# Sample's value products alternate the heads, and the layer norms' partial sums are added on VectorE

## The chip, the cores and the metric

The kernel runs on one core of a Trainium2 chip. The metric is the device time of one execution in microseconds. The engines are called by their names in the profile: PE (TensorE, matrix products; PEld its weight loads), DVE (VectorE), ACT (ScalarE), POOL (GpSimd) and SP (SyncE, which issues the DMAs). Each works through its own queue in program order, and semaphores order the queues against each other.

## What is computed

One step of a streaming encoder layer, for 512 prompt rows and 64 sample rows with a cache of 128 rows, model width 1024. Two groups of eight heads of width 64 attend: one with a forget gate and a causal mask, one over rows that an indexer picks. Then follow an output projection, a layer norm, a squared-ReLU feed-forward part of width 4096, a second layer norm and a gate.

```python
def layer_norm(x, g, b):
    mu = jnp.mean(xf, axis=-1, keepdims=True)
    var = jnp.mean(jnp.square(xf - mu), axis=-1, keepdims=True)
    return ((xf - mu) * lax.rsqrt(var + LN_EPS) * g + b).astype(x.dtype)
...
x = layer_norm(ALPHA * x + jnp.einsum('blm,md->bld', mix, w_o), ln1_g, ln1_b)
hid = jnp.square(jax.nn.relu(jnp.einsum('bld,df->blf', x, w_up)))
x = layer_norm(ALPHA * x + jnp.einsum('blf,fd->bld', hid, w_down), ln2_g, ln2_b)
```

Sample's attention of one head ends in probabilities (64 queries by 128 cached and 64 new rows) times values: `o = P[:, :128] @ V_cache + P[:, 128:] @ V_new`.

## The kernel before

All 576 rows lie along the free dimension and the 1024 features along the partitions, in eight blocks of 128: a tensor such as `Y` is [128, 8, 576]. Large products take float32 operands as a rounded part and a rest (`AH`/`AL`, `BH`/`BL`, the weights `whl`), three products for one; they are the products of line 273 in `gemm`. The products of the layer norms and of sample's attention take plain float32.

**Attention.** The projections of a pair of heads run on PE, and between their products the stages of the pair before are dealt out: scores (`qk`), bias and maximum, exponentials, transposes of the probabilities, values (`pv`), evacuation. The eight pairs are eight times the same pattern. `pv` writes one PSUM tile `V` (one buffer), head 0 to partitions 0 to 63, head 1 to 64 to 127. For the prompt (line 903) it alternates the heads inside the loop over key blocks. For the sample it does head 0, then head 1: each with a product over 128 cached rows (line 894, `Vc`) that begins the sum and one over 64 new rows (line 896, `vs`) that ends it.

**Layer norm.** The class `LayerNorm` does one half of the rows: L1A and L1B for the first norm (288 rows each, LN1), L2A (256) and L2B (320) for the second (LN2). A mean over features is a mean over 8 blocks and 128 partitions. `add` sums the blocks two by two into `self.s`, called `ln_s` in the profile, [128, 2, w], as they come out of the projection (lines 1100 and 1102, on DVE for L1A and the last pair, else on POOL); a product with the constant matrix `onesm` (1/1024 everywhere) sums over partitions and, with two accumulating products, over the two columns of partial sums:

```python
for x in range(2):
    PE.matmul(mu, onesm, self.s[:, x], start=(x == 0), stop=(x == 1))
```

`steps` then subtracts the mean in four steps (DVE, line 1128), squares (ACT, 1130 and 1133) and sums the squares into the same tile (line 1134, DVE or POOL). For the variance the tile is the weights of the product and one column of `onesm` streams through (line 1142), for each block of up to 128 rows and both partial sums. A square root (ACT), a reciprocal (DVE, 1148), a transpose that spreads the result over the partitions (line 55), scaling (1157) and the two parts `BH` (ACT, 1161) and `BL` (DVE, 1165) follow. The first half of `up(0)`, the up-projection, starts with these.

While L1A and L1B run, PE does the end of the output projection (`wo2`, evacuated by DVE at line 1208), then `ple` (products `g<-pT`, evacuated by ACT at line 1221), then `up(0)`; DVE also splits weights (line 179). In LN2 it is the last down-projection and the gate. A scheduler takes the operations in the order of the program and places them on the engines' queues by when it reckons their inputs ready, so that a change of one step can move its neighbours.

Of the kernel before, what the change touches and what calls it, by code (L numbers as in the profile page):

```python
# [11 lines left out]
OP = mybir.AluOpType  # L12
# [23 lines left out]
def tile_hybrid_step(ctx: ExitStack, tc: tile.TileContext, I, O):  # L36
    nc = tc.nc
    PE, ACT, DVE, POOL, SP = nc.tensor, nc.scalar, nc.vector, nc.gpsimd, nc.sync
# [4 lines left out]
    def f(ap):  # L43
        return ap.bitcast(F32)
# [5 lines left out]
    onesm = base.tile([128, 128], F32, name="onesm")  # L50
# [3 lines left out]
    def transpose(out, in_, n):  # L54
        PE.transpose(out, in_, ident[:n, :n])  # L55
# [58 lines left out]
    class Weights:  # L114
# [9 lines left out]
        def add(self, ap, pool_l=False, pair=None):  # L124
            aps = [ap] if pair is None else [ap, pair]
            n = 2 if pair is None else 7
            self.items.append(dict(aps=aps, h0=self.nh, n=n, pool=pool_l, left=None, when=0))
            self.nh += n
            return len(self.items) - 1
# [53 lines left out]
        def pieces_of(self, it, views):  # L183
# [24 lines left out]
            def add(x, out, a, b):  # L208
                return h0 + x, lambda: DVE.tensor_tensor(out, a, b, OP.add)

            t0 = add(3, tot[:, 0], b12, b22)
            t1 = add(2, tot[:, 1], b11, tot[:, 0])
            t2 = add(4, tot[:, 2], b21, tot[:, 1])
            t3 = add(5, b12, b12, b11)
# [83 lines left out]
    def psum_1(tag, bufs, dt=F32):  # L298
        return psA.tile([128, 512], dt, name=tag, tag="V" if tag == "V" else "R", bufs=1 if tag == "V" else 3)
# [586 lines left out]
    def pv(j):  # L886
        P = pair[j["p"]]
        ps = psum_1("V", 1)
        j["O"] = ps
        if j["s"]:  # L890
            g, pp = divmod(j["p"], 4)
            for hh in range(2):
                r = slice(hh * 64, hh * 64 + 64)
                PE.matmul(ps[r, :NS], Vc[g][:, (2 * pp + hh) * 64:(2 * pp + hh + 1) * 64], j["PT"][:, 0, r],
                          start=True, stop=False)
                PE.matmul(ps[r, :NS], P["vs"][:, r], j["PT"][:NS, 1, r], start=False, stop=True)
            return
        i = j["i"]
        for kb in range(i + 1):
            c = slice(0, 256) if kb < i else slice(128, 256)  # L900
            for hh in range(2):
                r = slice(hh * 64, hh * 64 + 64)
                PE.matmul(ps[r, c], P["vt"][:, kb, r], j["PT"][:, hh, kb, c], start=(kb == 0), stop=(kb == i))  # L903
# [16 lines left out]
    def jobs_of(p):  # L920
# [3 lines left out]
    PLAN = (((oevac, 5), (addmax, 1), (exp, 2), (make_bias, 0), (make_bias, -1)),  # L924
            ((ptrans, 3), (norm, 2)),
            ((qk, 0), (pevac, 3), (scales, 3), (pv, 4)))

    all_jobs = [j for p in range(8) for j in jobs_of(p)]
# [5 lines left out]
    def ticks(n):  # L934

        for _ in range(n):
            t = tick_no[0]
            tick_no[0] += 1
            for micro in PLAN:
                for stage, lag in micro:  # L940
                    j = job(t - lag)
                    if j and (j["close"] or stage not in (pv, oevac)) and not (stage is make_bias and "bias" in j):
                        stage(j)
                yield 1
# [132 lines left out]
    def psum_n():  # L1077
        return psN.tile([128, 512], F32, name="n", tag="n", bufs=2)
# [3 lines left out]
    class LayerNorm:  # L1082
# [10 lines left out]
        def add(self, j):  # L1093

            y = Y[:, :, self.sl]
            self.sums = j
            if j == 0:
                self.s = fb.tile([128, 2, 320], F32, name="ln_s", tag="ln_s" if self.sl.start else "relu", bufs=1 if self.sl.start else 2)[:, :, :self.w]
            elif j == 2:
                (DVE if self.sl is A else POOL).tensor_tensor(self.s, y[:, 0:2], y[:, 2:4], OP.add)  # L1100
            else:
                (DVE if j == 6 or self.sl is A else POOL).tensor_tensor(self.s, self.s, y[:, j:j + 2], OP.add)

        def pump(self):
            return next(self.gen, 0)
# [9 lines left out]
        def steps(self):  # L1115
            sl, gi, w = self.sl, self.gi, self.w
            y = Y[:, :, sl]
            while self.sums < 6:
                yield 1
            for _ in range(self.waits[0]):  # L1120
                yield 1
            mu = psum_n()[:, :w]
            for x in range(2):
                PE.matmul(mu, onesm, self.s[:, x], start=(x == 0), stop=(x == 1))  # L1124
            mb = mu[:, None, :].to_broadcast([128, 2, w])
            ss = self.s
            for j in range(0, 8, 2):
                DVE.tensor_tensor(y[:, j:j + 2], y[:, j:j + 2], mb, OP.subtract)
                if j == 0:
                    ACT.activation(ss, y[:, 0:2], AF.Square)  # L1130
                else:
                    sq = fb.tile([128, 2, 320], F32, name="ln_sq", bufs=2)[:, :, :w]
                    ACT.activation(sq, y[:, j:j + 2], AF.Square)
                    (DVE if j == 6 or sl is A else POOL).tensor_tensor(ss, ss, sq, OP.add)
                yield 1
            for _ in range(self.waits[1]):
                yield 1
            blks = [(c, min(128, w - c)) for c in range(0, w, 128)]
            var = psum_n()
            for i, (c, n) in enumerate(blks):  # L1140
                for x in range(2):
                    PE.matmul(var[:n, i:i + 1], ss[:, x, c:c + n], onesm[:, 0:1], start=(x == 0), stop=(x == 1))
            rt = fb.tile([128, 4], F32, name="ln_r", bufs=2)
            for i, (c, n) in enumerate(blks):
                if i == 0 or n < 128:
                    m = len(blks) - (blks[-1][1] < 128) if i == 0 else i + 1
                    ACT.activation(rt[:n, i:m], var[:n, i:m], AF.Sqrt, bias=epst[:n, 0:1])
                    DVE.reciprocal(rt[:n, i:m], rt[:n, i:m])
            for _ in range(self.waits[2]):
                yield 1  # L1150
            rb = psum_n()[:, :w]
            for i, (c, n) in enumerate(blks):
                transpose(rb[:, c:c + n], rt[:n, i:i + 1].to_broadcast([n, 128]), n)

            def scale(j):
                for x in (j, j + 1):
                    DVE.scalar_tensor_tensor(y[:, x], y[:, x], gb[:, gi, x:x + 1], rb, op0=OP.mult, op1=OP.mult)

            def high(j):
                for x in (j, j + 1):  # L1160
                    ACT.activation(BH[:, x, sl], y[:, x], AF.Identity, bias=gb[:, gi + 1, x:x + 1])

            def low(j):
                for x in (j, j + 1):
                    DVE.scalar_tensor_tensor(BL[:, x, sl], y[:, x], gb[:, gi + 1, x:x + 1], f(BH[:, x, sl]),
                                             op0=OP.add, op1=OP.subtract)
                self.ready += 1

            def bias(j):
                for x in (j, j + 1):  # L1170
                    ACT.activation(y[:, x], y[:, x], AF.Identity, bias=gb[:, gi + 1, x:x + 1])

            scale(0)
            high(0)
            yield 1
            scale(2)
            high(2)
            low(0)
            yield 1
            for j in (4, 6):  # L1180
                scale(j)
                high(j)
                yield 1
                low(j - 2)
                yield 1
            low(6)
            yield 1
            for _ in range(self.waits[3]):
                yield 1
            for j in range(0, 8, 2):  # L1190
                bias(j)
                yield 1

    def wo2(hs, ln, steps):
        for j in range(0, 8, 2):
            m = psum_g()
            for x in range(2):
                cs = slice((j + x) * 128, (j + x + 1) * 128)
                for k in (6, 7):
                    W = unit_w(U["ok", k], U["ok", 6])  # L1200
                    for _ in gemm(m[:, x, :HW], W, (0,), BH[:, k:k + 1], BL[:, k:k + 1], hs,
                                  first=(k == 6), last=(k == 7), wc=cs):
                        pass
                WT.step(steps)
                yield 1

            def ev(j=j, m=m):
                DVE.tensor_tensor(Y[:, j:j + 2, hs], m[:, :, :HW], Y[:, j:j + 2, hs], OP.add)
                ln.add(j)
            later(0, ev)  # L1210
# [341 lines left out]
```

## Time and profile before

| | before |
|---|---|
| median of 3 runs, us | 805.97 (805.49 to 806.9) |
| profiled execution, us | 805.3 |
| its span, us | 803.6 |
| granted TensorE clock | 1.00 in all stretches |
| records of sample's value products | 32 (line 894) and 32 (line 896) |
| records of the mean and the variance | 16 (line 1124) and 44 (line 1142) |

A row of the timeline has the start, the time from the first start to the last end, the engine, the line, the operation, output and inputs with shapes, and the number of records that it merges; for a product "128*64" is the part of the array used, rows by columns. In square brackets stands the idle time of the engine before it and who ended it. A row of the stretches has the stretch and its length, then busy time (and records) of PE, PEld, DVE, ACT and POOL, the clock and the use of DMA.

### The profile page before, as it was taken

What the parts mean: (1) busy time and instruction counts of PE and PEld (TensorE: products, weight loads), DVE (VectorE), ACT (ScalarE), POOL (GpSimd) and SP (SyncE); (2) the same over time, 40 slices, a digit from 0 to 9 for tenths busy, and PEclk for the clock granted to TensorE, in tenths of its full rate; (3) what the DMA queues carried; (4) which work ended last, traced back from release to release, by engine and by line L of the source; (5) the groups of instructions that cost most, each with busy time, mean ns of one, the idle gap of its engine ahead of it and who ended that gap; (6) DMA issues with size and microseconds to landing.
All of it is one profiled execution on the core that took longest, in us unless ns stands there. A gap on an engine that the chain in (4) does not pass through costs nothing.

```text
span 803.6 us, 14983 instructions
## 1 busy us (share of the span) xinstructions
PE 790.7 (98%) x5916; PEld 761.6 (95%) x5916; DVE 538.7 (67%) x1098; ACT 430.0 (54%) x905; POOL 120.0 (15%) x117
## 2 busy tenths in 40 slices
PE   7999999999999999999999999999999999999997
PEld 7988898999999999999999999999999999999997
DVE  6689999554456554989755858577594765647553
ACT  5568665767767544497424427154372534626351
POOL 8203435354332000110000000000000000012200
PEclk9999999999999999999999999999999999999999
DMA  8436233253222223442412314132231422630001
GB/s 295 167 55 151 90 106 94 87 191 122 86 72 84 73 73 117 151 163 60 125 53 80 105 53 131 53 106 82 77 106 53 132 80 79 245 109 27 27 28 65
DMA packets 30214, 81.44 MB, mean 101 GB/s; under 512 B 5056, under 2 KB 8896, under 8 KB 30016
## 3 DMA queue, kind: packets, MB, share of 16 engines
q1 hardware_dynamic: 30144, 80.49, 31.8%
q8 instruction: 46, 0.75, 0.4%
q14 instruction: 24, 0.20, 0.1%
HBM read 66.38 MB, written 9.54 MB: 94 GB/s over the span
## 4 chain that ended last, share of the span: by engine, by line
PE 86%; DVE 6%; issue 5%; ACT 1%; POOL 1%; DMA 0%; DVEq 0%; ACTq 0%; POOLq 0%
PE g L273 54%; PE m L273 17%; PE n L273 2%; PE V L903 2%; PE T L55 2%; DVE m L632 1%; DVE dbias L634 1%; PE S L818 1%; PE S L820 1%; PE m L413 1%; PE X L55 1%; PE S L420 1%; PE m L420 1%; PE n L1124 0%; DVE whl L179 0%
## 5 line engine op out<-in xcount | busy, mean ns | idle before, releaser
L175 ACT CAST whl<-wraw 128x512 fp32r<-128x512 f32 (+1 forms) x214 | 127.6, 611 | 142.4 <-PE g L273 116.2
L273 PE MATMUL g<-BH,whl 128*128 128x288 f32 (+2 forms) x864 | 181.9, 297 | 0.1
L273 PE MATMUL m<-AH,whl 128*128 128x288 f32 x736 | 177.9, 309 | 0.0
L179 DVE TENSOR_TENSOR whl<-wraw,whl 128x512 fp32r<-128x512 f32 (+1 forms) x180 | 121.3, 696 | 54.4 <-ACT whl L175 51.7
L273 PEld LDWEIGHTS g<-BH,whl 128*128 128x128 f32 x864 | 141.1, 188 | 2.4 <-ACT u L1318 1.2
L273 PEld LDWEIGHTS m<-AH,whl 128*128 128x128 f32 x736 | 126.3, 188 | 3.6 <-issue 2.2
L273 PE MATMUL g<-BL,whl 128*128 128x288 f32 (+2 forms) x432 | 127.2, 295 | 0.0
L273 PE MATMUL m<-AL,whl 128*128 128x288 f32 x368 | 109.0, 296 | 0.0
L273 PE MATMUL g<-hidE,whl 128*128 128x288 f32 (+2 forms) x768 | 103.4, 295 | 0.0
L273 PE MATMUL g<-hidO,whl 128*128 128x288 f32 (+2 forms) x768 | 103.4, 295 | 0.0
L273 PEld LDWEIGHTS g<-hidO,whl 128*128 128x128 f32 x768 | 102.4, 188 | 0.0
L273 PEld LDWEIGHTS g<-hidE,whl 128*128 128x128 f32 x768 | 102.2, 188 | 0.1
L273 PEld LDWEIGHTS g<-BL,whl 128*128 128x128 f32 x432 | 81.3, 188 | 0.1
L273 PEld LDWEIGHTS m<-AL,whl 128*128 128x128 f32 x368 | 69.6, 189 | 0.4
L273 PE MATMUL g<-s,whl 128*128 128x288 f32 x432 | 68.5, 298 | 0.0
L273 PEld LDWEIGHTS g<-s,whl 128*128 128x128 f32 x432 | 60.1, 188 | 2.2 <-DVE u L1320 1.2
L1100 POOL TENSOR_TENSOR ln_s<-Y 128x576 f32<-128x576 f32 (+2 forms) x3 | 4.6, 1544 | 383.8 <-DVE Y L1382 371.4
L179 POOL TENSOR_TENSOR whl<-wraw,whl 128x512 fp32r<-128x512 f32 x34 | 44.9, 1320 | 82.5 <-ACT whl L175 67.0
L836 ACT ACTIVATE sP<-sP,st 128x128 f32<-128x128 f32 (+4 forms) x72 | 39.6, 551 | 29.9 <-DVE st L828 29.3
L175 ACT CAST whl<-wsum 128x512 fp32r<-128x512 f32 x36 | 22.2, 616 | 60.7 <-PE g L273 60.5
L1357 DVE SCALAR_TENSOR_TENSOR Y<-Y,g 128x576 f32<-128x576 f32 x48 | 36.1, 751 | 24.5 <-PE g L273 24.0
L273 PE MATMUL m<-BH,whl 128*128 128x288 f32 x192 | 43.5, 304 | 0.0
(275 smaller groups left out, 1273.7 us busy)
## 6 DMA issues: line engine op xcount, KB each, us to landing
wraw<-in_w_up_dram SPq DMA_DIRECT2D x32, 512.0 KB, 3.5
wraw<-in_w_down_dram SPq DMA_DIRECT2D x32, 512.0 KB, 3.5
wraw<-in_w_qkv_dram SPq DMA_DIRECT2D x23, 512.0 KB, 4.1
wraw<-in_w_gate_dram SPq DMA_DIRECT2D x8, 512.0 KB, 4.6
wraw<-in_w_o_dram SPq DMA_DIRECT2D x8, 384.0 KB, 3.0
out_vT_dram<-v SPq DMA_DIRECT2D x8, 288.0 KB, 2.3
Y<-in_xT_dram SPq DMA_DIRECT2D x8, 288.0 KB, 5.5
PLD<-PL SPq DMA_DIRECT2D x4, 576.0 KB, 2.8
```

Source lines behind the costliest of these rows:

```text
L55: PE.transpose(out, in_, ident[:n, :n])
L175: ACT.copy(self.hv[h][0], src)
L179: eng.tensor_tensor(lv, src, f(hv), OP.subtract)
L273: PE.matmul(ps, W(w, kw, wc), a[:, ka, cols], start=(first and i == 0), stop=(last and i == n - 1))
L413: PE.matmul(mk[:, h, :HW], w0(part, k), a[:, k, h * HW:(h + 1) * HW], start=(k == 0 and i == 0), stop=(k == 7 and i == 2))
L420: PE.matmul(acc[b][:n[b], :304], a[:, k, b * 128:b * 128 + n[b]], ixw(part, k), start=(k == 0 and i == 0), stop=(k == 7 and i == 2))
L632: DVE.max(m, s)
L634: DVE.match_replace(out=s, in_to_replace=m, in_values=s, imm_value=GONE)
L818: PE.matmul(ps[:, :n], Q[:, c], K[:, :n], start=True, stop=False)
L836: ACT.activation(j["P"], j["P"], AF.Exp, bias=j["st"][:, 0:1], scale=-1.0, accum_out=s)
L903: PE.matmul(ps[r, c], P["vt"][:, kb, r], j["PT"][:, hh, kb, c], start=(kb == 0), stop=(kb == i))
L1357: later(0, lambda y=y, m=m, s=s: DVE.scalar_tensor_tensor(y, y, s, m[:, :, :HW], op0=OP.mult, op1=OP.add))
```

## The change

In sample's `pv` the two products over cached rows come first, head 0 and head 1, then the two over new rows. In `LayerNorm` a `fold` on DVE adds the second column of partial sums to the first, once when the sum of the rows is complete and once when the sum of squares is; the mean and each block of the variance then take one product in place of two.

```diff
-            for hh in range(2):
-                r = slice(hh * 64, hh * 64 + 64)
+            rs = [slice(hh * 64, hh * 64 + 64) for hh in range(2)]
+            for hh, r in enumerate(rs):
                 PE.matmul(ps[r, :NS], Vc[g][:, (2 * pp + hh) * 64:(2 * pp + hh + 1) * 64], j["PT"][:, 0, r],
                           start=True, stop=False)
+            for r in rs:
                 PE.matmul(ps[r, :NS], P["vs"][:, r], j["PT"][:NS, 1, r], start=False, stop=True)
...
+            if j == 6:
+                self.fold(self.s)
+
+        def fold(self, s):
+            DVE.tensor_tensor(s[:, 0], s[:, 0], s[:, 1], OP.add)
...
             mu = psum_n()[:, :w]
-            for x in range(2):
-                PE.matmul(mu, onesm, self.s[:, x], start=(x == 0), stop=(x == 1))
+            PE.matmul(mu, onesm, self.s[:, 0], start=True, stop=True)
...
                     (DVE if j == 6 or sl is A else POOL).tensor_tensor(ss, ss, sq, OP.add)
+                if j == 6:
+                    self.fold(ss)
                 yield 1
...
-                for x in range(2):
-                    PE.matmul(var[:n, i:i + 1], ss[:, x, c:c + n], onesm[:, 0:1], start=(x == 0), stop=(x == 1))
+                PE.matmul(var[:n, i:i + 1], ss[:, 0, c:c + n], onesm[:, 0:1], start=True, stop=True)
```

Lines behind the first edit move by one, lines behind `fold` by five or six: 1100 becomes 1101, 1124 becomes 1129, 1128 becomes 1133, 1134 becomes 1139, 1142 becomes 1148, 1208 becomes 1214; the fold is line 1108.

On PE, at sample's value products of a pair (`V` the output, `PTs` the transposed probabilities; a product's shape is that of its output):

```order
 L818 MATMUL S<-kO,qO 128x256
 L820 MATMUL S<-KLP_141,fox 128x256
-L894 MATMUL V<-PTs,Vc 64x64
-L896 MATMUL V<-PTs,vs 64x64
-L894 MATMUL V<-PTs,Vc 64x64
-L896 MATMUL V<-PTs,vs 64x64
+L894 MATMUL V<-PTs,Vc 64x64 x2
+L897 MATMUL V<-PTs,vs 64x64 x2
 L273 MATMUL m<-AH,whl 128x288
 L273 MATMUL m<-AL,whl 128x288
```

Only the order inside the group changes; it is so in all eight pairs.

On DVE in LN1, from the step after L1A's sum is complete to the sums of L1B, before the change (`ln_s_4135` is L1A's tile, `ln_s_4209` L1B's, `g_...` results of the output projection, `n_4225` L1A's mean):

```order
L1208 TENSOR_TENSOR Y_2740<-g_4201,Y_2740 128x2x288
L179 TENSOR_TENSOR whl_4167<-wraw_4111,whl_4167 128x512
L1128 TENSOR_TENSOR Y_2740<-Y_2740,n_4225 128x2x288 x2
L1208 TENSOR_TENSOR Y_2740<-g_4216,Y_2740 128x2x288
L1128 TENSOR_TENSOR Y_2740<-Y_2740,n_4225 128x2x288
L1134 TENSOR_TENSOR ln_s_4135<-ln_s_4135,ln_sq_4237 128x2x288
L1128 TENSOR_TENSOR Y_2740<-Y_2740,n_4225 128x2x288
L1134 TENSOR_TENSOR ln_s_4135<-ln_s_4135,ln_sq_4250 128x2x288
L1208 TENSOR_TENSOR Y_2740<-g_4240,Y_2740 128x2x288
L1134 TENSOR_TENSOR ln_s_4135<-ln_s_4135,ln_sq_4260 128x2x288
L1102 TENSOR_TENSOR ln_s_4209<-ln_s_4209,Y_2740 128x2x288
```

and the same place of the changed kernel (`ln_s_4210` is L1B's tile there, `n_4226` L1A's mean):

```order
L1214 TENSOR_TENSOR Y_2740<-g_4202,Y_2740 128x2x288
L1108 TENSOR_TENSOR ln_s_4135<-ln_s_4135 128x288
L179 TENSOR_TENSOR whl_4167<-wraw_4111,whl_4167 128x512
L1214 TENSOR_TENSOR Y_2740<-g_4217,Y_2740 128x2x288
L1133 TENSOR_TENSOR Y_2740<-Y_2740,n_4226 128x2x288 x4
L1139 TENSOR_TENSOR ln_s_4135<-ln_s_4135,ln_sq_4237 128x2x288
L1214 TENSOR_TENSOR Y_2740<-g_4240,Y_2740 128x2x288
L1139 TENSOR_TENSOR ln_s_4135<-ln_s_4135,ln_sq_4250 128x2x288
L1103 TENSOR_TENSOR ln_s_4210<-ln_s_4210,Y_2740 128x2x288
L1139 TENSOR_TENSOR ln_s_4135<-ln_s_4135,ln_sq_4260 128x2x288
L1108 TENSOR_TENSOR ln_s_4210<-ln_s_4210 128x288
L1108 TENSOR_TENSOR ln_s_4135<-ln_s_4135 128x288
```

The fold of L1A's sum stands two steps behind the end of that sum; the four subtractions now stand together, ahead of all sums of squares; the last evacuation of the output projection (of `g_4240`) is one place nearer to the mean; and two folds end the stretch.

On PE, where L1B's mean and L1A's variance stand among the products of `ple`, before:

```order
L273 MATMUL g_4297<-pT_3485,whl_4101 128x288
L1124 MATMUL n_4292<-ln_s_4209,onesm_61 128x288 x2
L273 MATMUL g_4297<-pT_3485,whl_4101 128x288 x2
L1142 MATMUL n_4316<-onesm_61,ln_s_4135 128x1 x4
L1142 MATMUL n_4316<-onesm_61,ln_s_4135 32x1 x2
L273 MATMUL g_4332<-pT_3485,whl_4101 128x288 x3
```

and in the changed kernel:

```order
L273 MATMUL g_4330<-pT_3485,whl_4101 128x288
L1129 MATMUL n_4294<-ln_s_4210,onesm_61 128x288
L1148 MATMUL n_4317<-onesm_61,ln_s_4135 128x1 x2
L1148 MATMUL n_4317<-onesm_61,ln_s_4135 32x1
L273 MATMUL g_4330<-pT_3485,whl_4101 128x288 x2
```

The variance of L1A now follows the mean of L1B directly. Counted in products of line 273 along PE's queue, L1A's mean stands eight later than before, L1B's mean nine later, and L1B's variance at the same place; so 56 such products stand between the two means (55 before) and 50 between L1B's mean and its variance (59 before). In LN2 the products stand where they stood.

## The prediction

> **What bounds the kernel.** I read the page's busy shares and its chain first, then the table of stretches, then the waits of TensorE.
>
> ```profile
> PE 790.7 (98%) x5916; PEld 761.6 (95%) x5916; DVE 538.7 (67%) x1098; ACT 430.0 (54%) x905; POOL 120.0 (15%) x117
> PE 86%; DVE 6%; issue 5%; ACT 1%; POOL 1%; DMA 0%; DVEq 0%; ACTq 0%; POOLq 0%
> 80.00:316.00 236.00, 234.94 (x1819) 217.17 (x1817) 149.70 (x409) 148.65 (x364) 72.99 (x60) 1.00 0.31 98
> 330.00:363.00 33.00, 32.45 (x243) 31.29 (x243) 29.26 (x58) 26.16 (x56) 5.33 (x4) 1.00 0.38 136
> PE g L273 <- DVE Y L1208: 0.4, 1, 0.4
> ```
>
> TensorE is busy 98% of the span and carries 86% of the chain that ended last. In the attention stage (80 to 316 us) it misses one us of 236, so time cut from its instructions there comes off the end. The stretch 330 to 363, which holds the first layer norm (LN1, halves A and B), is different: VectorE (third busy figure) is busy 29.26 of 33 us, and the one wait of TensorE on VectorE for a projection result falls there. An average would hide that; the two stages are costed apart.
>
> **Sample's value products.** One group of eight records (a plain float32 product shows as two records, called passes here), between two ordinary products:
>
> ```profile
> 313.06 0.29 PE L273 MATMUL m<-BH,whl 128*128 128x288 f32 x1
> 313.28 0.33 PE L894 MATMUL V<-PTs,Vc 128*64 128x64 f32 x2
> 313.54 0.33 PE L896 MATMUL V<-PTs,vs 64*64 64x64 f32 x2
> 313.79 0.33 PE L894 MATMUL V<-PTs,Vc 128*64 128x64 f32 x2
> 314.05 0.33 PE L896 MATMUL V<-PTs,vs 64*64 64x64 f32 x2
> 314.31 0.40 PE L273 MATMUL m<-BH,whl 128*128 128x288 f32 x1
> L894 PE MATMUL V<-PTs,Vc 128*64 128x64 f32 x32 | 5.3, 246 | 0.0
> ```
>
> Starts are what counts; durations overlap. The group takes 314.31 - 313.28 = 1.03, 0.26 for each pair of passes. What do the columns alone cost? The mean's products of the last norm half (320 columns, four passes) tell:
>
> ```profile
> 749.87 1.24 PE L1124 MATMUL n<-ln_s,onesm 128*128 128x320 f32 x4
> 750.70 0.52 PE L273 MATMUL g<-BH,whl 128*128 128x256 f32 x1
> 751.06 0.28 PE L273 MATMUL g<-BL,whl 128*128 128x256 f32 x1
> 355.81 9.30 PE g L273 x69
> ```
>
> An ordinary 288-wide product takes 9.30 / 69 = 0.135, a 256-wide one scaled from it 0.12. From 749.87 to 751.06 is 1.19; less the one product in between, 1.07 for four passes, 0.83 ns per column and pass. Two passes of 64 columns are then 0.11, and 0.15 of each 0.26 is a pause. It comes at each change of the used part of the array (128\*64, 64\*64, 128\*64, 64\*64, 128\*128). Where the part keeps its size and only the head changes, there is none:
>
> ```profile
> 78.71 0.87 PE L903 MATMUL V<-PT,vtok 128*64 128x256 f32 x8
> 79.51 0.40 PE L273 MATMUL m<-AH,whl 128*128 128x288 f32 x1
> 83.33 0.44 PE L810 MATMUL S<-KcT,q32s 64*64 64x128 f32 x4
> 83.60 0.29 PE L811 MATMUL S<-k32s,q32s 64*64 64x64 f32 x4
> 83.82 0.40 PE L273 MATMUL m<-AH,whl 128*128 128x288 f32 x1
> ```
>
> The prompt's value products alternate the heads: eight passes, by the order four of 256 and four of 128 columns, would take 1.28 one after another, and the next product starts 0.80 later. So two heads run side by side. The sample's score products do too: four passes of 128 columns, 0.43 in a row, are followed after 0.27.
>
> After the change a group is four passes at 128\*64, then four at 64\*64: two pauses fewer. With both heads side by side each four cost 0.11 and a pause, 0.26, so the group costs 0.52 and saves 0.51; heads in a row cost 0.21 + 0.15 each, 0.73, and save 0.30. L894's 32 records are eight groups: **4.1 us**, or 2.4. The row of L811 bounds it above: four passes and the change after them took 83.82 - 83.60 = 0.22, so 0.59 per group, 4.7. Below, zero, if the pause is not the change of part but L896 adding to what L894 has just written; a loss is excluded, as passes and operands are the same and L903 already runs so. I take 4.1, the nearest to L903. The Trainium skill ("TensorEngine Tiling (Array Packing)", Key Properties) says that changing the tiling mode drains the engine, while the tiles of one mode work independently; L903 and L810 agree, and by that rule zero is unlikely.
>
> **Means and variances.**
>
> ```profile
> L1124 PE MATMUL n<-ln_s,onesm x16: 377/406/432, 328.6 to 750.7; 128*128 128x288 f32 x8, 128*128 128x256 f32 x4, 128*128 128x320 f32 x4
> L1142 PE MATMUL n<-onesm,ln_s x44: 164/250/250, 338.8 to 762.8; 128*128 128x1 f32 x32, 128*32 128x1 f32 x8, 128*64 128x1 f32 x4
> 338.79 1.16 PE L1142 MATMUL n<-onesm,ln_s 128*128 128x1 f32 x12
> 339.89 2.25 PE L273 MATMUL g<-pT,whl 128*128 128x288 f32 x15
> 761.71 1.27 PE L1142 MATMUL n<-onesm,ln_s 128*128 128x1 f32 x12
> 762.91 0.38 PE L273 MATMUL g<-BH,whl 128*128 128x256 f32 x1
> ```
>
> Each norm half loses two passes of its mean: 0.48 at 288 columns (twice), 0.43 at 256, 0.53 at 320. Of the variance it loses half: 1.10 / 2 = 0.55 in each LN1 half, 1.20 / 2 = 0.60 in the last, and for eight passes at that 0.10 each 0.80 / 2 = 0.40. LN1: 0.96 + 1.10 = 2.06; LN2: 0.96 + 1.00 = 1.96, from which I take 1.9 for what of a block doesn't halve.
>
> Added are eight folds on VectorE, 128 rows by 256 to 320. The nearest rows and LN2's slack:
>
> ```profile
> 796.21 0.49 DVE L1459 TENSOR_TENSOR relu<-relu,PL 128x320 f32<-128x320 f32 x1 [1.42 <-ACT relu L1456]
> 715.73 0.69 DVE L1102 TENSOR_TENSOR ln_s<-ln_s,Y 128x512 f32<-128x512 f32 x1
> 719.13 1.02 PE L1124 MATMUL n<-ln_s,onesm 128*128 128x256 f32 x4
> ```
>
> 0.49 for 320, so 0.45 for 288. In LN2 the sum is ready at 716.42 and used at 719.13; VectorE's 2.7 us hide the fold there. Without that cover it would cost 0.45 each.
>
> **LN1, where the cover is thin.**
>
> ```profile
> 328.60 1.13 PE L1124 MATMUL n<-ln_s,onesm 128*128 128x288 f32 x4
> 329.02 0.68 DVE L179 TENSOR_TENSOR whl<-wraw,whl 128x512 fp32r<-128x512 f32 x1
> 332.00 1.45 POOL L1102 TENSOR_TENSOR ln_s<-ln_s,Y 128x576 f32<-128x576 f32 x1 [0.98 <-DVE Y L1208]
> 332.43 1.63 DVE L1134 TENSOR_TENSOR ln_s<-ln_s,ln_sq 128x576 f32<-128x576 f32 x1
> 335.99 0.74 DVE L1134 TENSOR_TENSOR ln_s<-ln_s,ln_sq 128x576 f32<-128x576 f32 x1
> 336.12 1.58 PE L273 MATMUL g<-pT,whl 128*128 128x288 f32 x10 [0.40 <-DVE Y L1208]
> 337.54 1.15 PE L1124 MATMUL n<-ln_s,onesm 128*128 128x288 f32 x4
> 345.81 0.76 DVE L1134 TENSOR_TENSOR ln_s<-ln_s,ln_sq 128x576 f32<-128x576 f32 x1 [1.89 <-POOL ln_s L1134]
> 346.83 1.62 PEld L273 LDWEIGHTS g<-pT,whl 128*128 128x128 f32 x12 [0.38 <-ACT PL L1221]
> 348.52 1.16 PE L1142 MATMUL n<-onesm,ln_s 128*128 128x1 f32 x12
> ```
>
> Mean A: the fold takes the place of L179 at 329.02 and ends by 329.47. By the order the mean stands eight products later, 328.60 + 8 x 0.135 = 329.68: no wait. Behind it in VectorE's queue stand the weight split and the evacuations of the output projection.
>
> Mean B: from mean A TensorE needs 337.54 - 328.60 = 8.94, less the wait of 0.40, less 0.48, plus one product more: 8.2. VectorE must in that time wait for mean A (some 0.7), then do four subtractions, five steps (three sums of squares, an evacuation, B's sum) and both folds: 9 x 0.67 (half of L1134's clash aside, steps of 0.74 start 0.67 apart) + 0.9 + 0.7 = 7.6. It fits, and the evacuation that TensorE waited for now stands ahead of these sums, so I take the 0.40 as gone.
>
> Variance B: its input was ready at 346.57, 9.03 after mean B's start, and was used 10.98 after it. TensorE's way shrinks: 0.48 of the mean, 0.55 of variance A, nine products (1.2) that the order now places ahead of mean B, and the 0.38 of the load queue if it goes: 8.4. The other way keeps 9.0 (0.48 less, 0.45 more). So a **new wait** of about 0.65 appears, with all products of the gated up-projection queued behind it. LN1 nets 2.06 + 0.40 + 0.38 - 0.65, about 2.2; I take **2.0**, with 0 and 2.7 as ends.
>
> **Sum.** 4.1 + 2.0 + 1.9 = 8.0. The profiled execution took 805.3 (span 803.6), so 797.3 for it; the median of the runs shown, 805.97, is 0.67 above, which gives **798.0**.
>
> **Rivals.**
> - *Heads in a row*: the two heads' passes write one V tile and the 64\*64 products share their rows, and run one after the other. For: no row shows this shape. Against: L903. 2.4 for 4.1, so 799.7. Chance 0.17.
> - *LN1 decided by VectorE, GpSimd and ScalarE*: L1134 took 1.63 at 332.43 where 0.74 is usual; it ended with GpSimd's L1102, also an addition of two operands. If a fold or a sum meets such an addition, 0.89 more each, two of them use up LN1's 2.0: 800.0. For: VectorE 29.26 of 33 us. Against: four subtractions, which have one operand in PSUM, now cover that addition. Chance 0.12. The Trainium skill ("SBUF — State Buffer", Who interferes with whom) says that a VectorE instruction with two SBUF inputs and a GpSimd one that reads SBUF block each other for a whole instruction; the row agrees.
> - *The pause stays*, being a wait on the accumulation or on the V tile: the group saves nothing, 802.1. For: the pause also stands between L894 and L896 of one head. Against: L903 accumulates without it. Chance 0.05.
> - *Slower*: every fold is late for its product, since it stands in VectorE's queue behind whatever is late there: 0.45 plus the clash of 0.89, eight times, 10.7 more, 808.7. It decides from where a fold ends after its product's turn; LN2's slack of 2.7 speaks against half of it. Chance 0.04.
> - *Better*: 4.7 and no new wait in LN1: 796.7. Chance 0.07.
>
> **How the numbers follow.** The forecast has 0.55. The range 796.6 to 801.2 takes in the first two rivals, the better case and most of their mixtures, and leaves out the other two. A measurement tells some 0.2%, 1.6 us, from no change: faster 0.91 (all but the slower case and a nearly lost gain), same 0.05, slower 0.04.
>
> **What would show it.** Right: a group of L894 and L897 in about 0.5 us, four records each with one pause between and one after; 8 records at the mean and 22 at the variance; eight more VectorE instructions of about 0.45. TensorE's wait at mean B is gone and one near 0.65 stands at variance B. Wrong: a group of 0.7 (heads in a row) or 1.0 (pause not from the change of part); waits on a fold over 2 us in LN1, or any in LN2.

## The result, and the profile after

The changed kernel takes **798.34 us** (median of 5 runs, 797.45 to 798.46) against 806.0 (median of 5, 805.49 to 806.9). The ratio is 0.990, with an interval of 0.9886 to 0.9915. The profiled execution of the changed kernel took 798.34, its span is 796.6.

Busy time and chain of waits, from the page of the changed kernel:

```profile
PE 783.7 (98%) x5886; PEld 756.2 (95%) x5886; DVE 541.3 (68%) x1106; ACT 429.6 (54%) x905; POOL 120.0 (15%) x117
PE 87%; DVE 9%; ACT 1%; issue 1%; DMA 1%; POOL 0%; DVEq 0%; ACTq 0%
```

PE has 30 records fewer (8 of the means, 22 of the variances) and DVE 8 instructions more, as the change says. PE still carries the chain, but DVE's share of it rose from 6% to 9%; this comes back below.

The last group of value products (timeline of PE; columns as in the prediction):

```profile
311.20 0.29 PE L273 MATMUL m<-BH,whl 128*128 128x288 f32 x1
311.42 0.34 PE L894 MATMUL V<-PTs,Vc 128*64 128x64 f32 x4
311.68 0.33 PE L897 MATMUL V<-PTs,vs 64*64 64x64 f32 x4
311.94 0.40 PE L273 MATMUL m<-BH,whl 128*128 128x288 f32 x1
```

From the group's first start to the next product it is 311.94 - 311.42 = 0.52, where it was 1.03. All eight groups read 0.52 or 0.53.

The first layer norm on PE, with the weight load that waited, and on DVE:

```profile
327.30 0.65 PE L1129 MATMUL n<-ln_s,onesm 128*128 128x288 f32 x2
335.39 0.65 PE L1129 MATMUL n<-ln_s,onesm 128*128 128x288 f32 x2
335.88 0.65 PE L1148 MATMUL n<-onesm,ln_s 128*128 128x1 f32 x6
336.46 2.25 PE L273 MATMUL g<-pT,whl 128*128 128x288 f32 x15
339.79 4.13 PE L273 MATMUL g<-pT,whl 128*128 128x288 f32 x30
344.00 0.76 PE L1148 MATMUL n<-onesm,ln_s 128*128 128x1 f32 x6
344.69 0.40 PE L273 MATMUL g<-BH,whl 128*128 128x288 f32 x1
```

```profile
344.00 0.67 PEld L1148 LDWEIGHTS n<-onesm,ln_s 128*128 128x128 f32 x6 [0.31 <-DVE ln_s L1108]
```

```profile
326.67 0.45 DVE L1108 TENSOR_TENSOR ln_s<-ln_s 128x288 f32<-128x288 f32 x1
334.60 0.82 DVE L1108 TENSOR_TENSOR ln_s<-ln_s 128x288 f32<-128x288 f32 x2
336.07 1.42 DVE L1133 TENSOR_TENSOR Y<-Y,n 128x576 f32<-128x576 f32 x2
342.40 0.76 DVE L1139 TENSOR_TENSOR ln_s<-ln_s,ln_sq 128x576 f32<-128x576 f32 x1 [1.90 <-POOL ln_s L1139]
343.07 0.51 DVE L1163 SCALAR_TENSOR_TENSOR Y<-Y,gb,n 128x288 f32<-128x288 f32 x1
343.50 0.45 DVE L1108 TENSOR_TENSOR ln_s<-ln_s 128x288 f32<-128x288 f32 x1
```

Both means have two passes in place of four and both variances six in place of twelve; each of these folds takes 0.45 or less. The two waits that stood in this stretch before (0.40 on DVE's evacuation, 0.38 of the load queue on ACT's) are gone from PE's and PEld's rows. One is new: the load for the variance of half B waits 0.31 for its fold.

**Where the time came from.** Two spans of one kernel also differ by their start: the first score products of the sample (line 810) begin at 83.33 in the trace before and at 84.47 in the one after, though nothing ahead of them was changed. So I cut every trace at three rows and compare the pieces: *attention* from that row of line 810 to the product behind the last group of value products, *LN1* from there to the first product of the up-projection behind the variance of half B, *rest* from there to the end of the span. For the kernel before, the third mark is

```profile
349.62 0.40 PE L273 MATMUL g<-BH,whl 128*128 128x288 f32 x1
```

| us | attention | LN1 | rest | sum |
|---|---|---|---|---|
| before | 314.31 - 83.33 = 230.98 | 349.62 - 314.31 = 35.31 | 803.6 - 349.62 = 453.98 | 720.27 |
| after | 311.94 - 84.47 = 227.47 | 344.69 - 311.94 = 32.75 | 796.6 - 344.69 = 451.91 | 712.13 |
| saved | 3.51 | 2.56 | 2.07 | 8.14 |

The later start takes 1.14 of the 8.14 back, and 803.6 - 796.6 = 7.0 is left between the two spans. The medians lie 7.66 apart. The pieces repeat from kernel to kernel within about 0.1 where the code is the same (next table), so they are a finer measure than the times.

### The profile page after: what moved, and what is told of

It is laid out like the page before. It is cut to its first block, busy times and chain, and to the rows that moved or that the text cites. A ratio compares the mean times of both kernels' runs of the same rounds, so it can differ in the third digit from the quotient of the medians.

```text
span 796.6 us, 14926 instructions
## 1 busy us (share of the span) xinstructions
PE 783.7 (98%) x5886; PEld 756.2 (95%) x5886; DVE 541.3 (68%) x1106; ACT 429.6 (54%) x905; POOL 120.0 (15%) x117
## 4 chain that ended last, share of the span: by engine, by line
PE 87%; DVE 9%; ACT 1%; issue 1%; DMA 1%; POOL 0%; DVEq 0%; ACTq 0%
PE g L273 55%; PE m L273 18%; PE n L273 2%; PE V L904 2%; DVE dbias L634 2%; DVE m L632 2%; PE T L55 2%; PE S L818 1%; PE S L820 1%; PE S L420 1%; PE m L413 1%; PE m L420 1%; PE X L55 1%; DVE dbias L612 1%; DVE sP L828 1%
```

## Experiments

Times are medians of 4 to 10 runs, the ratio is to the kernel before on the same chip; it reads 805.86 to 806.2 on the chips of these runs. The last two kernels leave out part of the indexer's choice.

| kernel | us | ratio, interval | attention | LN1 | rest |
|---|---|---|---|---|---|
| before / after | 806.0 / 798.34 | 0.9900 (0.9886 to 0.9915) | 230.98 / 227.47 | 35.31 / 32.75 | 453.98 / 451.91 |
| e1 value products only | 802.53 | 0.9955 (0.9943 to 0.9968) | 227.45 | 35.36 | 453.89 |
| e2 layer norms only | 801.55 | 0.9945 (0.9931 to 0.9958) | 230.97 | 32.74 | 451.99 |
| e3 crossed order | 801.84 | 0.9943 (0.9930 to 0.9955) | 230.97 | 32.74 | 452.01 |
| e4 padded to 128 rows | 797.01 | 0.9886 (0.9872 to 0.9899) | 226.46 | 32.76 | 451.92 |
| e5 LN1 without folds | 800.86 | 0.9935 (0.9922 to 0.9947) | 227.46 | 35.34 | 451.89 |
| e6 means only | 799.99 | 0.9924 (0.9911 to 0.9936) | 227.47 | 33.53 | 452.92 |
| e7 variances only | 800.33 | 0.9931 (0.9917 to 0.9944) | 227.47 | 34.31 | 452.90 |
| e8 padded, heads in a row | 797.22 | 0.9889 (0.9875 to 0.9902) | 226.50 | 32.76 | 451.91 |
| e9 before, less search | 805.57 | 0.9996 (0.9987 to 1.0005) | 230.43 | 35.34 | 453.93 |
| e10 after, less search | 796.61 | 0.9880 (0.9864 to 0.9897) | 226.44 | 32.75 | 451.92 |

**Theory**: three gains that add up, from pauses of the array, from products that are left out, and from waits that went with them. **Rivals**: the heads run in a row; the pause is a wait on the accumulation; LN1's gain is used up by VectorE.

### e1 and e2: each half of the change alone

e1 is the kernel before with the first hunk of the diff, e2 with the others.

> The kernel before with the new order of sample's value products alone. Theory (two pauses fewer per group, both heads side by side): a group takes 0.52 us instead of 1.03, eight groups 4.1 less, 801.9 beside a kernel before at 806.0. Rival (heads in a row): 0.73 per group, 803.6. Rival (the pause belongs to the accumulation): 1.03, 806.0.

> The kernel before with the folded sums of the layer norms alone. Theory: TensorE loses 2.06 us of products in LN1 and 1.96 in LN2 and gets one wait of some 0.3 us back at variance B, while two waits of 0.4 go: about 3.9 less, 802.1. Rival (LN1 is decided by VectorE, GpSimd and ScalarE, so that only LN2 saves): 804.0.

The halves add: attention falls by 3.5 in e1 alone, LN1 by 2.57 and the rest by 1.99 in e2 alone, and neither touches the other's piece. A group of e1 takes 311.55 - 311.02 = 0.53, so the heads run side by side. Both times missed what was expected by 0.6, e1 upward and e2 downward. In e1, 8 x 0.50 is 4.0, and attention gives 3.5: half a microsecond is missing. e9 and e10 are about that. In e2 it is LN1 that gives more, 2.57; e5 to e7 take that apart.

### e3: is it the change of the used part, or the accumulation?

```diff
+            old(0, start=True, stop=False)
+            new(1, start=True, stop=False)
+            old(1, start=False, stop=True)
+            new(0, start=False, stop=True)
```

`old(h)` is head h's product over the cached rows (`Vc`), `new(h)` the one over the new rows (`vs`).

> The changed kernel with a third order in the group: cached rows of head 0, new rows of head 1, cached rows of head 1, new rows of head 0. No product adds to what the one just before it has written, but the used part of the array changes at each. Theory (the pause belongs to the change of part): the group takes 1.03 again, 4.1 more than the changed kernel, about 802.4. Rival (the pause belongs to the accumulation): 0.52 to 0.73, 798.3 to 800.

The last group of e3 on PE:

```profile
314.43 0.33 PE L895 MATMUL V<-PTs,Vc 128*64 128x64 f32 x2
314.69 0.33 PE L899 MATMUL V<-PTs,vs 64*64 64x64 f32 x2
314.94 0.33 PE L895 MATMUL V<-PTs,Vc 128*64 128x64 f32 x2
315.20 0.33 PE L899 MATMUL V<-PTs,vs 64*64 64x64 f32 x2
315.45 0.40 PE L273 MATMUL m<-BH,whl 128*128 128x288 f32 x1
```

Here no product adds to what the one ahead of it wrote: the head changes each time. The group is at 315.45 - 314.43 = 1.02 and attention at 230.97, as before the change. The pause goes with the change of the used part (128\*64 to 64\*64 and back), not with the accumulation. The time, 801.84, is 0.6 below what was expected, by the same half microsecond of attention.

### e4 and e8: no change of the used part inside the group

Both set the 64 new rows in tiles of 128 rows with zeros below, so that every product of a group uses 128\*64. e4 keeps the new order, e8 the old one (head 0 complete, then head 1).

```diff
+            POOL.memset(pt_now["vs", p][NS:128], 0.0)
...
+                POOL.memset(pt_now["PTs"][NS:128, 1], 0.0)
...
-                PE.matmul(ps[r, :NS], P["vs"][:, r], j["PT"][:NS, 1, r], start=False, stop=True)
+                PE.matmul(ps[r, :NS], P["vs"][:, r], j["PT"][:, 1, r], start=False, stop=True)
```

> The changed kernel with the 64 new rows padded by zeros to 128 (two tiles zeroed once), so that all four products of a group use 128 rows by 64 columns. Theory (pause at the change of part, heads side by side): eight passes of 64 columns for two heads cost 0.21 and one pause 0.15, 0.37 per group instead of 0.52, 1.2 less than the changed kernel, 797.1. Rival (the accumulation pauses): 0.52, 798.3. Rival (heads in a row): 0.43 and 0.15, 0.58, 798.8.

> The changed kernel with the new rows padded to 128 as in the padded run, but the program's order as before the change: head 0 complete, then head 1. Theory (only a change of the used part pauses, and heads on different columns run side by side whatever their order): 0.37 per group, 797.0, as the padded run. Rival (the alternation is what lets them run side by side): 0.43 and one pause, 0.58, 798.7.

The last group of e4, and that of e8:

```profile
309.74 0.34 PE L900 MATMUL V<-PTs,Vc 128*64 128x64 f32 x4
309.91 0.29 PE L903 MATMUL V<-PTs,vs 128*64 128x64 f32 x4
310.12 0.40 PE L273 MATMUL m<-BH,whl 128*128 128x288 f32 x1
```

```profile
310.54 0.34 PE L900 MATMUL V<-PTs,Vc 128*64 128x64 f32 x4
310.71 0.29 PE L902 MATMUL V<-PTs,vs 128*64 128x64 f32 x4
310.93 0.40 PE L273 MATMUL m<-BH,whl 128*128 128x288 f32 x1
```

0.38 and 0.39: one pause less again, at 0.14. The products got larger and the group shorter. And the order of the heads makes no difference once the part stays the same: on PE's queue the head changes once in a group of e8, in e4 three times.

That e8's rows look like those of e4 needs a word. On PE's queue its group stands as in the kernel before: cached rows and new rows of head 0, then cached rows and new rows of head 1. A timeline has the records in order of their starts, and there the four passes over cached rows come first: they start at 310.54 and 310.55, then at 310.65 and 310.66. Head 1 thus begins 0.01 behind head 0, ahead of products that stand before it in the queue. So for the starts of PE's products on different columns it does not hold that an engine works through its queue in program order, as the beginning of this document has it.

So what the change gains at this place, it gains by putting products of one shape together; that it alternates the heads is how it does so. Attention is 1.01 (e4) and 0.97 (e8) shorter than in the changed kernel. e4 at 797.01 and e8 at 797.22 are the fastest complete kernels here; between them nothing can be told.

### e5, e6, e7: the layer norms in parts

e5 leaves LN1 as it was and folds in LN2 only (`if j == 6 and self.gi`); e6 folds for the means only, e7 for the variances only. The value products are as changed in all three.

> The changed kernel with the folds of LN1 taken back, those of LN2 kept. Theory (LN1 nets 2.0 to 2.3 us, as its waits go too): 800.3 to 800.6. Rival (VectorE's chain eats LN1's saving): 798.4, as the changed kernel.

> The changed kernel with the folds for the means alone; the variances take two products again. Theory: the means' products give 0.48 twice, 0.43 and 0.53, 1.9 below the kernel with the new order of the value products alone (802.5), so 800.6. Rival (a fold ahead of the mean is on the way of LN1): 801.6 or more.

> The changed kernel with the folds for the variances alone. Theory: 22 records at 0.10 each fewer, 2.1 below 802.5, 800.4, less some tenths if the fold at variance B is waited for. Rival (a product of one column costs only its column, 0.05): 1.1 less, 801.4.

Against e1's 802.53, e5 shows LN2's part as 1.67, and 800.86 - 798.34 = 2.52 as LN1's; by pieces 2.0 and 2.59. PEld in e7 (in e5 the same two rows read 0.63 and 0.39):

```profile
333.11 1.36 PEld L273 LDWEIGHTS g<-pT,whl 128*128 128x128 f32 x10 [0.64 <-DVE Y L1213]
343.33 1.62 PEld L273 LDWEIGHTS g<-pT,whl 128*128 128x128 f32 x12 [0.40 <-ACT PL L1226]
```

With the variances alone both old waits stay, and LN1 saves 35.31 - 34.31 = 1.00: the products. With the means alone PEld has neither wait, and LN1 saves 35.31 - 33.53 = 1.78, of which 0.96 are products. So the waits went with the means: with the fold at the mean the scheduler sets the mean's products, the subtractions and the evacuations in another order. The traces show it: in e6 half A's four subtractions stand together, as in the changed kernel, and 56 products lie between the two means; in e7 both are as before the change. Together it is 2.56 and not 2.78; the wait of 0.31 for a fold stands only in the kernel with both. e5 and e6 missed their expectations, by 0.3 above and 0.6 below: e5's took LN1 at 2.0 to 2.3, and e6's left out the waits that go with the means. e7 came within 0.1 of its own, so a pass of one column costs 0.10 here and not 0.05.

### e9 and e10: where half a microsecond of the attention went

In the trace after, PE waits longer at one place of the second pair than before, where the transposes of the sums of the softmax (line 55, output X) are queued behind ACT's work. Timeline of PE before, then after:

```profile
123.75 0.66 PE L55 MATMUL X<-ident,rows 128*128 128x128 f32 x4 [0.32 <-ACT vs L765]
```

```profile
124.88 0.66 PE L55 MATMUL X<-ident,rows 128*128 128x128 f32 x4 [0.70 <-ACT vs L765]
```

From the first score products to this row it is 123.75 - 83.33 = 40.42 before and 124.88 - 84.47 = 40.41 after, with the first of the eight groups in between: its 0.50 is gone again. PE's own rows show 0.38 of it, the growth of this wait from 0.32 to 0.70. In e4, whose group is shorter still, it is 40.42 too (83.66 to 124.08). The chain of waits names who sets this distance. Its shares for 98 to 126 us, after:

```profile
by line: DVE m L632 36.7%; DVE dbias L634 36.7%; DVE sP L828 11.3%; issue 4.6%; DVE qs L692 2.4%; PE X L55 2.3%; DVE mix L914 2.1%; PE V L904 2.1%; ACT whl L175 1.8%; ACT sP L836 0.8%; ACT vs L765 0.6%; DVE st L841 0.4%; DVE sums L844 0.4%;
```

Lines 632 and 634 are the indexer's search for the largest scores, which runs on VectorE in the first pairs; line 828, the maximum of a softmax row, stands in the same queue, ACT's exponentials wait for it, and PE for ACT. To test it, the search is cut short in both kernels:

```diff
-            for r in range(16 if i < 4 else 6):
+            for r in range(16 if i < 3 else 1):
```

> The kernel before, with 31 of the indexer's 86 search rounds... counted by tile: the 16 rounds over the widest tile (512 columns) and the 6 over the sample's tile (192) are cut to one each; what follows reads the tile as it then is, so this part of the choice is left out. In all eight traces so far the first score products of the sample (the record of line 810) and the transposes of the sums in the second pair (line 55, output X, waiting for ScalarE's line 765) stand 40.4 us apart, though the one group of value products between them took 1.03, 0.52 or 0.38. Theory: VectorE (26.2 of 27 us busy there, back to back with the search) sets that distance. Then it shrinks here by the wait of 0.32 that TensorE has there, to about 40.1, and the attention section (first score products to the product after the last group) from 230.98 to about 230.65 or less, where the search held others too. Rival: ScalarE's own queue or the weights' arrival sets it; then 40.4 and 230.98 stay.

> The changed kernel with the same rounds of the search left out. Theory (VectorE's search holds the second pair and eats the first group's 0.50): the wait of 0.70 goes, the distance falls from 40.4 to about 39.7, and the attention section is 8 x 0.50 = 4.0 us shorter than in the kernel before with the same cut, where without the cut it was 3.5. Rival (something else holds the second pair): the distance stays 40.4 and the difference of the sections 3.5.

(The count in the first expectation is wrong: the search has 3 x 16 + 6 = 54 rounds, and 20 are left out.) Busy times for 99 to 126 us (PE, PEld, DVE, ACT, POOL) of the changed kernel, then of e10, and the transposes in e10:

```profile
99.00:126.00 27.00, 26.30 (x206) 24.55 (x208) 26.21 (x75) 16.08 (x45) 10.78 (x10) 1.00 0.37 104
```

```profile
99.00:126.00 27.00, 27.00 (x215) 25.18 (x216) 20.40 (x64) 18.53 (x51) 11.67 (x11) 1.00 0.41 111
124.03 0.60 PE L55 MATMUL X<-ident,rows 128*128 128x128 f32 x4
```

VectorE falls from 26.21 of 27 us to 20.40, and PE is busy for the whole stretch: the wait is gone. The distance is 124.03 - 84.59 = 39.44 in e10 and 123.64 - 83.70 = 39.94 in e9, 0.50 apart where the kernels with the whole search were equal. They shrank by 0.97 and 0.48, more than the 0.70 and 0.32 that were expected from PE's rows; the load queue's rows have waits of 0.90 and 0.52 at the same place. Attention is 230.43 in e9 and 226.44 in e10: 3.99 us apart, all of 8 x 0.50. So VectorE's search holds the second pair, and with it the first group's gain was turned into waiting. What the cut gives the kernel before (230.98 - 230.43 = 0.55 in the trace) is too little for its time to show.

## Why the prediction was right

The forecast was 798.0 and the time is 798.34. The sum was 8.0 and the pieces give 8.14. Its terms were less exact: 0.59 too much for the value products, 0.56 too little for LN1 and 0.17 too little for LN2. The mechanisms hold, but that these errors nearly cancel is luck.

- **The value products, 4.1 forecast.** The group was forecast at 0.52 and is 0.52; two pauses fewer, heads side by side, four records at each line. The mechanism is shown by e1, e3, e4 and e8. The size was 0.6 too high: 3.51 came off the end. The step that failed is "it misses one us of 236, so time cut from its instructions there comes off the end". One of the few waits of that stage stands behind the first group, and it is not fixed in length: it is the rest up to a moment that VectorE sets. It grew from 0.32 to 0.70 and took one group's gain with it (e9, e10).
- **LN1, 2.0 forecast, 2.56 measured.** The waits of 0.40 and 0.38 went, as forecast; e6 and e7 show that the means took them along. The mean of half B came 335.39 - 327.30 = 8.09 behind that of half A, where 8.2 was reckoned. The products at the two variances were 0.58 and 0.69 instead of 1.10 each. The mis-sized term is the new wait at variance B: 0.31 in place of 0.65. The variance began 344.00 - 335.39 = 8.61 behind the mean, so PE's own way was 8.61 - 0.31 = 8.30 (8.4 reckoned), and the fold was done after 343.95 - 335.39 = 8.56, where 9.0 was reckoned. Before, DVE's subtractions for half B began 1.59 behind their mean's 337.54, because three weight splits of line 179 stood ahead of them in its queue. After the change only one does, and they begin 336.07 - 335.39 = 0.68 behind the mean, 0.43 sooner than the 0.48 of two passes alone explain. Before, then after:

```profile
337.32 1.88 DVE L179 TENSOR_TENSOR whl<-wraw,whl 128x512 fp32r<-128x512 f32 x3
339.13 1.41 DVE L1128 TENSOR_TENSOR Y<-Y,n 128x576 f32<-128x576 f32 x2
```

```profile
335.33 0.68 DVE L179 TENSOR_TENSOR whl<-wraw,whl 128x512 fp32r<-128x512 f32 x1
```

  ACT's first square followed the pair of subtractions sooner as well: 341.51 - 340.54 = 0.97 behind its end before, 338.08 - 337.49 = 0.59 after, by these rows of before and after:

```profile
341.51 0.68 ACT L1130 ACTIVATE ln_s<-Y 128x576 f32<-128x576 f32 x1
```

```profile
338.08 0.69 ACT L1135 ACTIVATE ln_s<-Y 128x576 f32<-128x576 f32 x1
```

  The prediction had let that way shrink by the passes alone. Lost on it again were 0.34, since the fold stands behind an instruction of line 1163 (343.07) in VectorE's queue. Together 9.0 - 0.43 - 0.38 + 0.34 = 8.53. With these sizes LN1 adds up to 0.96 (the means, as reckoned) + 0.93 (the variances) + 0.40 + 0.38 - 0.31 = 2.36; 0.20 of the 2.56 stays open. The first wait is 0.64 in the load queue's row, as in e7, where the prediction took PE's 0.40; at 0.64 the sum would be covered, but no run separates the two.
- **LN2, 1.9 forecast, 2.07 measured** in the piece from LN1 to the end. No wait on a fold appeared; the means account for 453.98 - 452.92 = 1.06 (e6), the variances for 1.08 (e7). In the last half the variance is

```profile
755.32 0.70 PE L1148 MATMUL n<-onesm,ln_s 128*128 128x1 f32 x6
755.95 0.39 PE L273 MATMUL g<-BH,whl 128*128 128x256 f32 x1
```

  0.63 long where it was 1.20, close to the half that was reckoned.
- **From the profiled execution to the median.** The prediction added 0.67, as the profiled run before was faster than its median. That was the right sign: its start was the earliest of all twelve traces (83.33, the others 83.66 to 84.59). That the start is what varies, the prediction did not know.
- **The rivals.** *Heads in a row* would have given groups of 0.73; all are 0.52 or 0.53. *The pause stays* falls by the groups' 0.52, and e3 shows that no accumulation is its cause. *LN1 decided by VectorE, GpSimd and ScalarE* falls by e5: without LN1's folds 2.5 us are lost. The additions of line 1139 on DVE in LN1 take 0.75 or 0.76 in the trace after; none meets an addition of GpSimd as line 1134 did before with 1.63. (That one did not end with GpSimd's addition, as the prediction says: it ended at 334.06, 0.61 behind the addition's end at 333.45.) After the change the two engines still meet once, where GpSimd's first addition for half B starts beside the fold and a weight split of line 179. Before, then after:

```profile
329.24 1.78 POOL L1100 TENSOR_TENSOR ln_s<-Y 128x576 f32<-128x576 f32 x1 [12.39 <-DVE Y L1208]
```

```profile
326.88 2.16 POOL L1101 TENSOR_TENSOR ln_s<-Y 128x576 f32<-128x576 f32 x1 [12.38 <-DVE Y L1214]
327.03 0.68 DVE L179 TENSOR_TENSOR whl<-wraw,whl 128x512 fp32r<-128x512 f32 x1
```

  GpSimd's addition took 2.16 in place of 1.78 and ended 329.04 - 327.71 = 1.33 behind the split, before 331.02 - 329.70 = 1.32 behind it. The Trainium skill's rule on that pair ("SBUF — State Buffer", Who interferes with whom), that a VectorE instruction with two inputs in SBUF and a GpSimd one that reads SBUF contend, agrees with these rows. PE waited for neither of them.

  *Slower* falls by the result; only one of eight folds is late, by 0.31. *Better* asked for 4.7 from the groups; that is what padding approaches (8 x 0.65 = 5.2 in e4 at the groups, 4.52 in attention).

  On the value products the rule of the Trainium skill ("TensorEngine Tiling (Array Packing)", Key Properties), that a change of the tiling mode drains the engine, agrees with e3, e4 and e8; the price in these traces is 0.14 to 0.15 for each change.

## What to carry to other kernels

Count the changes of the used part of the array between small products: products of one shape belong together, and filling a short contraction with zeros can be cheaper than a product of another size. Where PE is busy 98% of the time, look for the few waits that are left before taking a saving at full size: a gain ahead of a wait whose end another engine sets is waited away, and the chain of waits of that stretch names the engine. Cut the traces at the same rows in both kernels and compare the pieces; the whole time hides both the missing half microsecond and a start that varies more than that.

## What was not expected of the hardware

- A product over 128 rows, half of them zeros, costs less than one over 64 rows when its neighbours use 128: 0.38 for a group in place of 0.52.
- Two heads on different columns run side by side also when the program has them one after the other (e8, 0.39 for eight passes; at 0.83 ns per column they would take 0.43 in a row, without any pause). They start out of the order of PE's queue then.
- The start varies. The first products follow each other at about 0.25 us, later ones of the same kinds at 0.13 to 0.14. The short step sets in at about 8.3 us in the trace before and only after 10.9 us in the one after. PEld before, then after:

```profile
8.08 0.29 PEld L420 LDWEIGHTS m<-iw,AH 128*128 128x128 f32 x1
8.32 0.19 PEld L420 LDWEIGHTS S<-iw,AH 128*128 128x128 f32 x1
8.46 0.19 PEld L420 LDWEIGHTS X<-iw,AH 128*128 128x128 f32 x1
```

```profile
10.44 0.33 PEld L420 LDWEIGHTS X<-iw,AL 128*128 128x128 f32 x1
10.69 0.22 PEld L420 LDWEIGHTS S<-iw,AH 128*64 128x64 f32 x1
10.94 0.42 PEld L413 LDWEIGHTS m<-AH,whl 128*128 128x128 f32 x2
11.31 0.19 PEld L413 LDWEIGHTS m<-AL,whl 128*128 128x128 f32 x1
11.44 0.32 PEld L413 LDWEIGHTS m<-AH,whl 128*128 128x128 f32 x2
```

  The granted clock reads 1.00 in both in each microsecond from 6 to 12, so what delays the short step is not shown by these traces. The first score products of the sample start up to 84.59 - 83.33 = 1.26 us apart over the twelve traces.
